# State space mixer: output computed by features, heads in pairs on column halves, decay and skip as loaded tiles

## The chip, the cores and the metric

One core of a Trainium2 chip runs the whole program. The metric is the device time of one execution in microseconds; of several executions the median is taken.

## The reference, cut to what matters

Two transformer-like blocks run one after the other on a sequence of 1024 tokens with 1024 features, all in float32. The second block projects its input to three mixers (attention, a state space mixer, a gated linear recurrence), joins their outputs and projects back. The change is in the state space mixer (SSD): 16 heads of 64 features, in two groups of eight, a state of 128, and the sequence in 8 chunks of 128 tokens.

```
xdt = xh * dt
lmat = exp(where(causal, a_cs[l] - a_cs[s], -inf))        # per head, 128 x 128
cb = einsum('bclgn,bcsgn->bcgls', cc, bc)                 # per group
y_diag = einsum('bcgels,bcsgep->bclgep', cb * lmat, xdt)  # inside the chunk
states = einsum('bclgn,bcgel,bclgep->bcgepn', bc, decay_states, xdt)
y_off = einsum('bclgn,bcgepn,bcgel->bclgep', cc, prev_states, exp(a_cs))  # from earlier chunks
y = y_diag + y_off + xh * d_skip
```

`y` is then gated with silu(z), normalised by groups, and goes with the other mixers' outputs into the last projection.

## The kernel before

**How the work is ordered.** Each stage is a Python generator. Two calls of `weave` (line 146) run the generators against a small planner clock: a generator yields the TensorE time that it has just emitted and a time for which it wants to wait, and the planner takes the first one in its list that is ready. `ssd` stands first in the second list, ahead of `project2`, which emits the remaining big projections (`qkv(1)`, then the gates and the recurrence). So chunks of the mixer are laid between projection matmuls. A tile scheduler may then move an instruction to another place in the order of its engine where its data are ready earlier; each engine and each DMA queue works off its own order.

**Buffers.** Tiles come from pools of fixed slots: 28 `u` (128x1024 float32), 7 `ub` (128x1392), 5 `f` (128x512), 8 PSUM banks, and for weights 3 `raw`, 4 `whi`, 4 `wlo`. `need(...)` lets a generator wait until so many slots are free in the order of emission; a freed slot goes to the end of the list. A weight tile is loaded to `raw` on SP's queue (line 227) and split in a high part (ACT, line 215) and a low part (POOL or DVE, line 212); each wide projection matmul (128x512) is made three times with these parts.

**Before the mixer.** `steps` (1714) computes the step sizes and the running sums `acs` by token, and from them `eacs` (half of exp(acs)), `dtd` and `eend`; it also transposes the sums to `rest` (16 rows per chunk by token) and writes them in parts to DRAM (`seg_l`, `seg_r`). `ssd_tail` (1839) finishes one 128-feature tile of the convolved input at a time: silu, four and four transposes to token order, and for the eight feature tiles of x a write of the token-ordered copy to `xtm_dram` (1859).

**One chunk of `ssd`** (1886 to 1990), token by token order:
- loads: `xt` (128 tokens x 1024 features, 512 KB, line 1896), `rl` and `rr` (1898, 1899); `xdt` = x times the step on POOL (1902), with 32 zeroed columns behind (1901);
- `pcb` (1905) is the product of B and C of each group; `pseg` (1916, 1920) and an exponential on ACT (1921) give the decay matrices `lt`, which DVE multiplies with `pcb` (1924);
- POOL makes `xdec` (1930) and multiplies `xt` by the skip factors in place (1931);
- `pyo` (1939, not in chunk 0): C stationary, the state of eight heads moving, one 128x512 float32 matmul per group; DVE multiplies by `eacs` (1941) and adds the skip part (1943);
- `pyd` (1951): for each head `lt` (128x128) stationary and 96 columns of `xdt` moving, of which 64 are wanted; DVE adds four heads at a time (1953);
- `pst` (1963) updates the state (1966, 1969);
- `pyt2` (1982): eight transposes turn the chunk's 1024 features to feature order, ACT copies them (1983), and ACT's queue writes them to `yraw_dram` (1985).

In the trace a float32 matmul or weight load appears as two records; a transpose as one. Another stage, `sgu_mixer`, already has float32 matmuls with 64 stationary columns and 128 moving ones, whose outputs go by turns to PSUM partitions 0 to 63 and 64 to 127 (line 1084):

```
for j in range(2):
    pe.matmul(p[64 * j:64 * j + 64, n, :], vn[q][:, n, gi * 64:(gi + 1) * 64], swt[:, gi, :],
              start=True, stop=True)
```

Of the kernel before, what the change touches and what calls it, by code (L numbers as in the profile page):

```python
# [75 lines left out]
def tile_block(ctx: ExitStack, tc: tile.TileContext, A, out):  # L76
# [55 lines left out]
    def need(**n):  # L132
        while any(len(C[k].free) < x for k, x in n.items()):
            yield 0.0, 0.7
# [1570 lines left out]


    T_FD, T_XL, T_ZL, T_XBC, T_ZA, T_ZS = 0, 1, 5, 9, 21, 25
    sp = acs = eacs = dtd = eend = None
    negc = const.tile([128, 8, 8], F32, name="negc")
    negc_dram = dr.tile([64, 128], F32, name="negcd")  # L1710
    seg_l = dr.tile([6, 128 * 128], BF16, name="segl")
    seg_r = dr.tile([6, 128 * 128], BF16, name="segr")

    def steps():
        nonlocal sp, acs, eacs, dtd, eend
        sp = small("sp", [128, 8, 24], bufs=2, tag="s5x")
        acs = small("acs", [128, 8, 24], bufs=2, tag="s5x")
        eacs = small("eacs", [128, 8, 16], bufs=2, tag="s5z")
        dtd = small("dtd", [128, 8, 16], bufs=2, tag="s5z")
        eend = small("eend", [128, 8, 16], bufs=1, tag="s5si")  # L1720
        tri = small("tri", [128, 128], tag="s5y")
# [72 lines left out]
        rest = st_[:, 4, 0:128]  # L1794
        v.tensor_copy(rest, pr_[:, 128:256])  # L1795
        free(pr_)
        s.activation(eacs[:], acs[:, :, 8:24], AF.Exp)
        s.activation(eend[:], endb[:, :, 8:24], AF.Exp)
        v.tensor_tensor(dtd[:], endb[:, :, 8:24], acs[:, :, 8:24], op=ALU.subtract)
        s.activation(dtd[:], dtd[:], AF.Exp)  # L1800
        v.tensor_tensor(dtd[:], dtd[:], sp[:, :, 8:24], op=ALU.mult)
        v.tensor_scalar(eacs[:], eacs[:], 0.5, None, op0=ALU.mult)

        sq128 = lambda d, r: d[r].rearrange("(a b) -> a b", a=128)
        for j in range(3):
# [28 lines left out]
        return x  # L1834

    xtm_dram = dr.tile([SEQ, 1024], F32, name="xtm")
    bfm, btm, cfm = {}, {}, {}

    def ssd_tail(i, x):
        yield from need(f=2)  # L1840
        for hf in range(2):
            t = f512("th")
            s.activation(t[:], half(x, hf), AF.Tanh, scale=0.5)
            v.scalar_tensor_tensor(half(x, hf), t[:], 1.0, half(x, hf), op0=ALU.add, op1=ALU.mult)
            free(t)
        yield 0.0, 8.0
        if i < 10:
            yield from need(u=1)
            xs_ = u("xst", (128, 8, 128))
            for q in range(2):  # L1850
                yield from need(ps=1)
                p = bank("ptt", (128, 4, 128))
                for c in range(4):
                    pe.transpose(p[:, c, :], x[:, (4 * q + c) * 128:(4 * q + c + 1) * 128], ident[:])
                s.activation(xs_[:, 4 * q:4 * q + 4, :], p[:], AF.Copy, scale=0.5)
                free(p)
                yield 0.5, 0.0
        if i < 8:
            nc.scalar.dma_start(xtm_dram[:].rearrange("(c p) f -> p c f", p=128)[:, :, i * 128:(i + 1) * 128], xs_[:])
            free(x, xs_)  # L1860
        elif i < 10:
            bfm[i - 8], btm[i - 8] = x, xs_
        else:
            cfm[i - 10] = x
        done.add(f"xbc{i}")
# [20 lines left out]
    def ssd():  # L1886
# [4 lines left out]
        bch = lambda x: x.unsqueeze(2).to_broadcast([128, 16, 64])  # L1891
        for c in range(8):
            tk = slice(c * 128, (c + 1) * 128)
            yield from need(ub=4, u=3, f=1, ps=2)
            xt = ub("xt", (128, 1024))
            nc.sync.dma_start(xt[:], xtm_dram[tk, :])
            rl, rr = ub("rl", (6, 2048), BF16), ub("rr", (6, 2048), BF16)
            nc.sync.dma_start(rl[:], seg_l[:, c * 2048:(c + 1) * 2048])
            nc.sync.dma_start(rr[:], seg_r[:, c * 2048:(c + 1) * 2048])
            xdt = ub("xdt", (128, 1056))  # L1900
            g.memset(xdt[:, 1024:1056], 0.0)
            g.tensor_tensor(h64(xdt[:, 0:1024]), h64(xt[:]), bch(sp[:, c, 8:24]), op=ALU.mult)
            pcb = bank("pcb", (128, 2, 128))
            for gi in range(2):
                pe.matmul(pcb[:, gi, :], bfm[gi][:, tk], cfm[gi][:, tk], start=True, stop=True)
            cb_ = f512("cbs")
            cbs = cb_[:, 0:256].rearrange("p (g l) -> p g l", g=2)
            s.activation(cbs, pcb[:], AF.Copy, scale=0.25)
            free(pcb)
            lt = []  # L1910
            for gi in range(2):
                lt.append(u("lt", (128, 8, 128)))
                for b in range(2):
                    yield from need(ps=1)
# [12 lines left out]
            xdec = None  # L1927
            if c < 7:
                xdec = u("xdec")
                g.tensor_tensor(h64(xdec[:]), h64(xt[:]), bch(dtd[:, c]), op=ALU.mult)  # L1930
            g.tensor_tensor(h64(xt[:]), h64(xt[:]), bch(hrow[:, 2, 8:24]), op=ALU.mult)
            yield 0.5, 6.0
            yield from need(u=1)
            yt = u("yt")
            for gi in range(2):
                if c:
                    yield from need(ps=1)
                    pQ = bank("pyo", (128, 8, 64))
                    pe.matmul(pQ[:].rearrange("p h d -> p (h d)"), cfm[gi][:, tk],
                              state[:, gi].rearrange("p h d -> p (h d)"), start=True, stop=True)  # L1940
                    v.tensor_tensor(h64(half(yt, gi)), pQ[:],
                                    eacs[:, c, 8 * gi:8 * gi + 8].unsqueeze(2).to_broadcast([128, 8, 64]), op=ALU.mult)
                    v.tensor_tensor(half(yt, gi), half(yt, gi), half(xt, gi), op=ALU.add)
                    free(pQ)
                    yield 0.9, 0.0
            for q in range(4):
                yield from need(ps=1)
                pN = bank("pyd", (128, 4, 96))
                for j in range(4):
                    h = 4 * q + j  # L1950
                    pe.matmul(pN[:, j, :], lt[h // 8][:, h % 8, :], xdt[:, h * 64:h * 64 + 96], start=True, stop=True)  # L1951
                yq = h64(yt[:, q * 256:(q + 1) * 256])
                v.tensor_tensor(yq, yq if c else h64(xt[:, q * 256:(q + 1) * 256]), pN[:, :, 0:64], op=ALU.add)
                free(pN)
                if q == 1:
                    yield 1.8, 0.0
            free(xt, xdt, lt)
            yield 1.8, 0.0
            if c < 7:
                for gi in range(2):  # L1960
                    yield from need(ps=1)
                    pS = bank("pst2", (128, 8, 64))
                    pe.matmul(pS[:].rearrange("p h d -> p (h d)"), btm[gi][:, c, :], half(xdec, gi),
                              start=True, stop=True)
                    if c:
                        g.tensor_tensor(state[:, gi], state[:, gi],
                                        eend[:, c, 8 * gi:8 * gi + 8].unsqueeze(2).to_broadcast([128, 8, 64]),
                                        op=ALU.mult)
                        v.tensor_tensor(state[:, gi], state[:, gi], pS[:], op=ALU.add)
                    else:  # L1970
                        v.tensor_copy(state[:, gi], pS[:])
                    free(pS)
                free(xdec)
                yield 1.8, 2.0
            yield from need(u=1)
            ys = u("ys", (128, 8, 128))
            for q in range(2):
                yield from need(ps=1)
                p = bank("pyt2", (128, 4, 128))
                for j in range(4):  # L1980
                    k = 4 * q + j
                    pe.transpose(p[:, j, :], yt[:, k * 128:(k + 1) * 128], ident[:])
                s.activation(ys[:, 4 * q:4 * q + 4, :], p[:], AF.Copy)
                free(p)
            nc.scalar.dma_start(yraw_dram[:].rearrange("(k p) t -> p k t", p=128)[:, :, tk], ys[:])
            free(yt, ys)
            yield 0.9, 0.0
        free(state, *bfm.values(), *btm.values(), *cfm.values())
        done.add("ssd")

# [604 lines left out]
```

## Time and profile before

| | us |
|---|---|
| median of 3 runs | 2401.92 |
| lowest and highest | 2399.53, 2407.82 |
| the profiled execution | 2402.67 |
| its span, first to last instruction | 2400.8 |

The span is what the profile divides into shares. The profiled execution's own time is 1.9 us more than its span and 0.75 us above the median of the runs. `PE` is TensorE's matmuls, `PEld` its weight loads (they lie beside the matmuls), `DVE`, `ACT` and `POOL` the other engines, `SP` a queue that issues DMAs. A matmul record's length includes its way through the array; what matmuls cost one after another is read from the distance of their starts.

### The profile page before, as it was taken

To read this page: it belongs to the slowest core of one execution; us is meant where nothing else is said; L and a number is where in the kernel's file an instruction comes from. 1 tells how busy PE (TensorE), PEld (TensorE's weight loads), DVE (VectorE), ACT (ScalarE), POOL (GpSimd) and SP (SyncE) were. 2 spreads that over 40 slices of the span, in tenths; PEclk is the share of its full clock that TensorE was granted. 3 is DMA by queue.
4 is the path that set the end of the run, shared out by engine and by line. 5 is a ranking of instruction groups with operands and counts; after the bars stand their busy time and mean duration, and the time that the engine had idled before them with its cause. 6 is when DMAs were issued, how large, how long until landed. Compare 5 with 4: busy or idle time off the path is not lost.

```text
span 2400.8 us, 29770 instructions
## 1 busy us (share of the span) xinstructions
PE 2260.8 (94%) x11002; PEld 1795.4 (75%) x11002; DVE 1217.6 (51%) x2148; ACT 795.5 (33%) x1425; POOL 945.5 (39%) x855
## 2 busy tenths in 40 slices
PE   5898789797999999999999998999999999999998
PEld 2787657575678888888888876787777777778877
DVE  8689644886961202021212785766644585662111
ACT  2423222443342121212112354334333354543322
POOL 4465534747553232222324543123652233120543
PEclk7999889799999999999999999999999999999999
DMA  7311444344222111111112334232344433231564
GB/s 270 94 48 58 134 150 158 113 159 140 72 87 66 49 49 46 51 40 53 49 58 83 110 115 145 70 94 88 110 146 144 168 110 136 67 115 63 155 190 141
DMA packets 144194, 251.68 MB, mean 105 GB/s; under 512 B 15720, under 2 KB 51240, under 8 KB 144048
## 3 DMA queue, kind: packets, MB, share of 16 engines
q1 hardware_dynamic: 110960, 209.25, 27.2%
q10 hardware_dynamic: 30816, 32.76, 4.1%
q0 software_dynamic: 2272, 7.77, 1.0%
q8 instruction: 86, 1.41, 0.2%
q14 instruction: 60, 0.49, 0.1%
HBM read 200.20 MB, written 48.48 MB: 104 GB/s over the span
## 4 chain that ended last, share of the span: by engine, by line
PE 69%; DVE 15%; DMA 5%; issue 3%; POOL 3%; ACT 3%; SPq 1%; DVEq 0%; ACTq 0%; POOLq 0%
PE pf L255 6%; PE pf L251 6%; PE pf L253 6%; PE pz L251 6%; PE pz L253 6%; PE pz L255 6%; PE pg L238 3%; PE pg L239 3%; PE pg L240 3%; PE pO L2331 2%; DVE cv L809 2%; PE pfo L238 2%; PE pfo L239 2%; PE pfo L240 2%; PE pyd L1951 1%
## 5 line engine op out<-in xcount | busy, mean ns | idle before, releaser
L212 POOL TENSOR_TENSOR wlo<-raw,whi 128x512 fp32r<-128x512 f32 (+1 forms) x285 | 397.3, 1396 | 868.0 <-ACT whi L215 839.2
L215 ACT ACTIVATE whi<-raw 128x512 fp32r<-128x512 f32 (+1 forms) x432 | 267.0, 622 | 1019.0 <-PE pf L253 295.1
L212 DVE TENSOR_TENSOR wlo<-raw,whi 128x512 fp32r<-128x512 f32 (+1 forms) x147 | 115.9, 789 | 364.8 <-ACT whi L215 364.4
L255 PE MATMUL pf<-h,wlo 128*128 128x512 f32 x704 | 231.8, 392 | 5.2 <-DVE wlo L212 2.9
L251 PE MATMUL pf<-h,whi 128*128 128x512 f32 x704 | 231.9, 392 | 0.1
L253 PE MATMUL pf<-h,whi 128*128 128x512 f32 x704 | 231.9, 392 | 0.0
L251 PE MATMUL pz<-u,whi 128*128 128x512 f32 x512 | 170.1, 399 | 0.9 <-DVE sptmp L1795 0.6
L253 PE MATMUL pz<-u,whi 128*128 128x512 f32 x512 | 168.2, 394 | 0.0
L255 PE MATMUL pz<-u,wlo 128*128 128x512 f32 x512 | 166.8, 394 | 0.0
L255 PEld LDWEIGHTS pf<-h,wlo 128*128 128x128 f32 x704 | 132.5, 188 | 36.0 <-DVE wlo L212 3.7
L251 PEld LDWEIGHTS pf<-h,whi 128*128 128x128 f32 x704 | 132.4, 188 | 29.6 <-ACT whi L215 0.5
L253 PEld LDWEIGHTS pf<-h,whi 128*128 128x128 f32 x704 | 132.5, 188 | 29.3
L239 PE MATMUL pg<-wlo,act 128*128 128x512 f32 x352 | 138.3, 393 | 0.9 <-DVE wlo L212 0.5
L238 PE MATMUL pg<-whi,act 128*128 128x512 f32 x352 | 137.1, 393 | 0.4 <-ACT whi L215 0.4
L240 PE MATMUL pg<-whi,act 128*128 128x512 f32 x352 | 137.0, 392 | 0.0
L251 PEld LDWEIGHTS pz<-u,whi 128*128 128x128 f32 x512 | 95.8, 188 | 24.5 <-issue 1.9
L253 PEld LDWEIGHTS pz<-u,whi 128*128 128x128 f32 x512 | 96.0, 188 | 22.3 <-issue 1.2
L255 PEld LDWEIGHTS pz<-u,wlo 128*128 128x128 f32 x512 | 96.0, 188 | 21.9 <-issue 0.7
L1579 DVE TENSOR_TENSOR x<-x,pg 128x512 f32<-128x512 f32 x80 | 53.7, 685 | 109.3 <-PE pg L240 109.2
L239 PE MATMUL pfo<-wlo,mix 128*128 128x512 f32 x256 | 101.1, 396 | 0.5 <-POOL wlo L212 0.5
L1552 DVE TENSOR_TENSOR a<-a,pf 128x512 f32<-128x512 f32 x44 | 28.7, 683 | 143.0 <-PE pf L255 143.0
L240 PE MATMUL pfo<-whi,mix 128*128 128x512 f32 x256 | 100.5, 394 | 0.0
(641 smaller groups left out, 4968.9 us busy)
## 6 DMA issues: line engine op xcount, KB each, us to landing
raw<-in_w_ffn_in_dram SPq DMA_DIRECT2D x108, 256.0 KB
wm<-in_w_mod_dram SPq DMA_DIRECT2D x48, 512.0 KB
raw<-in_w_out_dram SPq DMA_DIRECT2D x96, 256.0 KB
raw<-in_w2f_dram SPq DMA_DIRECT2D x66, 256.0 KB
raw<-in_w_ffn_out_dram SPq DMA_DIRECT2D x56, 256.0 KB
raw<-in_w2q_dram SPq DMA_DIRECT2D x48, 256.0 KB
raw<-in_w_in_dram SPq DMA_DIRECT2D x36, 256.0 KB
mraw<-y2d SPq DMA_DIRECT2D x32, 256.0 KB
```

The lines of the kernel that those rows point to most:

```text
L212: (v if dve else g).tensor_tensor(lo, full, hi, op=ALU.subtract)
L215: s.activation(hi, full, AF.Copy)
L238: pe.matmul(p, lh, rh, start=start, stop=False)
L239: pe.matmul(p, lh, rl, start=False, stop=False)
L240: pe.matmul(p, ll, rh, start=False, stop=stop)
L251: pe.matmul(p, wh, xh[k], start=k == 0, stop=False)
L253: pe.matmul(p, wh, xl[k], start=False, stop=False)
L255: pe.matmul(p, wl, xh[k], start=False, stop=k == kt - 1)
L809: v.scalar_tensor_tensor(a3, *tap(k), a3, op0=ALU.mult, op1=ALU.add)
L1552: v.tensor_tensor(a_[:], a_[:], pair[1][hf][:], op=ALU.mult)
L1579: v.tensor_tensor(x, x, p[t][:], op=ALU.add)
L2331: pe.matmul(pO[:, b, :], x[:, jb % 2, b * 128:(b + 1) * 128], H["va"][:, o:o + 96], start=False, stop=jb == nj - 1 and b == 3)
```

## The change

The stationary and the moving operand change places, so that a chunk's result comes out with features on partitions and tokens along the row. `pyd` has 64 columns of `xdt` stationary and `lt` (128 tokens) moving; the two heads of a 128-feature tile write PSUM partitions 0 to 63 and 64 to 127. `pyo` becomes four matmuls of 128 state columns against C. The transposes and their copies go. The decay factor and the skip part are now needed with features on partitions: `steps` writes half of exp of the transposed sums to `ea_dram`, and each chunk loads `eb` from it (two DMAs that repeat 16 rows over 64 partitions each); `ssd_tail` scales the feature-ordered x by half the skip factor on ACT and writes it to `xd_dram`, and each chunk loads `xd`. A chunk asks for 6 `ub` slots, before 4.

```diff
@@ steps
-        s.activation(eacs[:], acs[:, :, 8:24], AF.Exp)
+        er = small("ear", [128, 128], tag="s5y")
+        s.activation(er[:], rest, AF.Exp)
+        v.tensor_scalar(er[:], er[:], 0.5, None, op0=ALU.mult)
+        nc.scalar.dma_start(ea_dram[:], er[:])
...
-        v.tensor_scalar(eacs[:], eacs[:], 0.5, None, op0=ALU.mult)
@@ before ssd_tail
+    dcol = const.tile([128, 8], F32, name="dcol")
+    for r in range(2):
+        v.tensor_scalar(dcol[64 * r:64 * r + 64, :], hrow[64 * r:64 * r + 64, 2, 8 + r:24:2], 0.5, None, op0=ALU.mult)
@@ ssd_tail
+            s.activation(x[:], x[:], AF.Copy, scale=dcol[:, i:i + 1])
+            nc.scalar.dma_start(xd_dram[i * 128:(i + 1) * 128, :], x[:])
@@ ssd
-            yield from need(ub=4, u=3, f=1, ps=2)
+            yield from need(ub=6, u=3, f=1, ps=2)
...
-            xdt = ub("xdt", (128, 1056))
-            g.memset(xdt[:, 1024:1056], 0.0)
-            g.tensor_tensor(h64(xdt[:, 0:1024]), h64(xt[:]), bch(sp[:, c, 8:24]), op=ALU.mult)
+            xdt = ub("xdt", (128, 1024))
+            xd, eb = ub("xd", (128, 8, 128)), ub("eb", (128, 8, 128))
+            nc.sync.dma_start(xd[:], xd_dram[:].rearrange("(k p) t -> p k t", p=128)[:, :, tk])
+            if c:
+                for r in range(2):
+                    nc.sync.dma_start(eb[64 * r:64 * r + 64], ea_dram[c * 16 + r:c * 16 + 16:2, :].unsqueeze(0)
+                                      .to_broadcast([64, 8, 128]))
+            g.tensor_tensor(h64(xdt[:]), h64(xt[:]), bch(sp[:, c, 8:24]), op=ALU.mult)
...
-            g.tensor_tensor(h64(xt[:]), h64(xt[:]), bch(hrow[:, 2, 8:24]), op=ALU.mult)
...
-                    pQ = bank("pyo", (128, 8, 64))
-                    pe.matmul(pQ[:].rearrange("p h d -> p (h d)"), cfm[gi][:, tk],
-                              state[:, gi].rearrange("p h d -> p (h d)"), start=True, stop=True)
-                    v.tensor_tensor(h64(half(yt, gi)), pQ[:],
-                                    eacs[:, c, 8 * gi:8 * gi + 8].unsqueeze(2).to_broadcast([128, 8, 64]), op=ALU.mult)
-                    v.tensor_tensor(half(yt, gi), half(yt, gi), half(xt, gi), op=ALU.add)
+                    pQ = bank("pyo", (128, 4, 128))
+                    for j in range(4):
+                        pe.matmul(pQ[:, j, :], state[:, gi, 2 * j:2 * j + 2].rearrange("p h d -> p (h d)"),
+                                  cfm[gi][:, tk], start=True, stop=True)
+                    v.tensor_tensor(yt[:, 4 * gi:4 * gi + 4], pQ[:], eb[:, 4 * gi:4 * gi + 4], op=ALU.mult)
                     free(pQ)
                     yield 0.9, 0.0
+                g.tensor_tensor(yt[:], yt[:], xd[:], op=ALU.add)
-            for q in range(4):
+            for gi in range(2):
                 yield from need(ps=1)
-                pN = bank("pyd", (128, 4, 96))
+                pN = bank("pyd", (128, 4, 128))
                 for j in range(4):
-                    h = 4 * q + j
-                    pe.matmul(pN[:, j, :], lt[h // 8][:, h % 8, :], xdt[:, h * 64:h * 64 + 96], start=True, stop=True)
-                yq = h64(yt[:, q * 256:(q + 1) * 256])
-                v.tensor_tensor(yq, yq if c else h64(xt[:, q * 256:(q + 1) * 256]), pN[:, :, 0:64], op=ALU.add)
+                    for r in range(2):
+                        h = 8 * gi + 2 * j + r
+                        pe.matmul(pN[64 * r:64 * r + 64, j, :], xdt[:, h * 64:h * 64 + 64], lt[gi][:, 2 * j + r, :],
+                                  start=True, stop=True)
+                y_ = slice(4 * gi, 4 * gi + 4)
+                v.tensor_tensor(yt[:, y_], yt[:, y_] if c else xd[:, y_], pN[:], op=ALU.add)
                 free(pN)
-                if q == 1:
-                    yield 1.8, 0.0
-            free(xt, xdt, lt)
-            yield 1.8, 0.0
+                yield 0.9, 0.0
+            free(xt, xdt, lt, xd, eb)
+            nc.scalar.dma_start(yraw_dram[:].rearrange("(k p) t -> p k t", p=128)[:, :, tk], yt[:])
...
-            ys = u("ys", (128, 8, 128))
-            for q in range(2):
-                p = bank("pyt2", (128, 4, 128))
-                for j in range(4):
-                    k = 4 * q + j
-                    pe.transpose(p[:, j, :], yt[:, k * 128:(k + 1) * 128], ident[:])
-                s.activation(ys[:, 4 * q:4 * q + 4, :], p[:], AF.Copy)
-            nc.scalar.dma_start(yraw_dram[:].rearrange("(k p) t -> p k t", p=128)[:, :, tk], ys[:])
-            free(yt, ys)
-            yield 0.9, 0.0
+            free(yt)
+            yield 0.1, 0.0
```

## Rows read from the trace of the kernel before

**Rows 1.** The page: busy time by engine, and the granted clock in 40 slices.

```profile
PE 2260.8 (94%) x11002; PEld 1795.4 (75%) x11002; DVE 1217.6 (51%) x2148; ACT 795.5 (33%) x1425; POOL 945.5 (39%) x855
...
PEclk7999889799999999999999999999999999999999
```

**Rows 2.** Busy time by stretch; after POOL come granted clock, DMA share, GB/s.

```profile
core 0: us, PE busy (x) PEld busy (x) DVE busy (x) ACT busy (x) POOL busy (x), PEclk, DMA share, GB/s
1637.00:1820.00 183.00, 182.47 (x986) 137.38 (x986) 98.62 (x142) 62.56 (x114) 94.25 (x80) 1.00 0.37 117
1820.00:2000.00 180.00, 177.72 (x737) 137.87 (x736) 120.50 (x123) 84.64 (x123) 53.15 (x40) 1.00 0.42 146
```

**Rows 3.** TensorE's waits in 1637 to 1820 us: us, times, longest.

```profile
PE pq L238 <- ACT cbs L1908: 0.5, 1, 0.5
```

**Rows 4.** The chain of waits, 1560 us to the end: start, us, what.

```profile
1674.25 3.54 PE pyd L1951 x32
...
1737.29 1.72 PE pyo L1939 x4
```

**Rows 5.** TensorE's timeline in chunk 1: start, us, line, operation, tiles.

```profile
1674.09 3.71 PE L1951 MATMUL pyd<-xdt,lt 128*128 128x96 f32 x32
1677.63 0.38 PE L1916 MATMUL pseg<-mask,identb 128*128 128x512 bf16 x1
...
1682.85 1.03 PE L1982 MATMUL pyt<-ident,yt 128*128 128x128 f32 x8
1683.64 0.47 PE L240 MATMUL pq<-whi,u 128*128 128x512 f32 x1
1683.96 0.39 PE L238 MATMUL pq<-whi,u 128*128 128x512 f32 x1
1684.18 0.60 PE L1905 MATMUL pcb<-xc 128*128 128x128 f32 x4
1684.55 0.48 PE L239 MATMUL pq<-wlo,u 128*128 128x512 f32 x1
1684.87 0.39 PE L240 MATMUL pq<-whi,u 128*128 128x512 f32 x1
```

**Rows 6.** Lines 1951 and 1982: count, duration ns min/median/max, first and last start.

```profile
L1951 PE MATMUL pyd<-xdt,lt x256: 243/275/275, 1651.9 to 1808.5; 128*128 128x96 f32 x128
...
L1982 PE MATMUL pyt<-ident,yt x64: 270/272/327, 1660.9 to 1812.8; 128*128 128x128 f32 x64
```

**Rows 7.** TensorE's timeline around line 1084, and that line's weight loads.

```profile
400.60 0.61 PE L255 MATMUL pz<-hh,wlo 128*128 128x512 f32 x2
401.15 1.09 PE L1084 MATMUL psg<-sw,vn 128*64 128x128 f32 x16
...
403.15 1.09 PE L1084 MATMUL psg<-sw,vn 128*64 128x128 f32 x16
404.18 0.73 PE L251 MATMUL pz<-hh,whi 128*128 128x512 f32 x2
404.75 0.62 PE L253 MATMUL pz<-hl,whi 128*128 128x512 f32 x2
...
L1084 PEld LDWEIGHTS psg<-sw,vn x64: 132/137/137, 401.1 to 410.1; 128*64 128x64 f32 x64
```

**Rows 8.** Groups of ACT, DVE, POOL in 1637 to 1820 us: busy, mean ns, idle.

```profile
L1983 ACT ACTIVATE ys<-pyt 128x512 f32<-128x512 f32 x16 | 8.8, 596 | 6.4 <-PE pyt L1982 6.4
...
L1943 DVE TENSOR_TENSOR yt<-yt,xt 128x512 f32<-128x512 f32 x14 | 15.0, 1080 | 2.7 <-POOL xt L1931 2.2
...
L1931 POOL TENSOR_TENSOR xt<-xt,hrow 128x1024 f32<-128x1024 f32 x7 | 14.2, 2028 | 0.2
...
L212 POOL TENSOR_TENSOR wlo<-raw,whi 128x512 fp32r<-128x512 f32 x20 | 25.8, 1295 | 54.7 <-ACT whi L215 54.7
```

**Rows 9.** SP's queue in 1637 to 1820 us, what it waited for: us, times, longest.

```profile
SPq L227 <- POOL wlo L212: 60.7, 16, 12.3
...
SPq L1896 <- PE pyd L1951: 6.2, 1, 6.2
```

**Rows 10.** DMA queue that ACT issues to, 1637 to 1820 us: packets, MB, share of 16 engines.

```profile
q10 hardware_dynamic: 9472, 6.31, 11.2%
```

More of the change, by code (lines that the diff above doesn't have):

```diff
@@ L1707, in tile_block @@
     T_FD, T_XL, T_ZL, T_XBC, T_ZA, T_ZS = 0, 1, 5, 9, 21, 25
-    sp = acs = eacs = dtd = eend = None
+    sp = acs = dtd = eend = None
     negc = const.tile([128, 8, 8], F32, name="negc")
@@ L1714, in steps @@
     def steps():
-        nonlocal sp, acs, eacs, dtd, eend
+        nonlocal sp, acs, dtd, eend
         sp = small("sp", [128, 8, 24], bufs=2, tag="s5x")
         acs = small("acs", [128, 8, 24], bufs=2, tag="s5x")
-        eacs = small("eacs", [128, 8, 16], bufs=2, tag="s5z")
         dtd = small("dtd", [128, 8, 16], bufs=2, tag="s5z")
@@ L1836, in tile_block @@
     xtm_dram = dr.tile([SEQ, 1024], F32, name="xtm")
+    xd_dram = dr.tile([1024, SEQ], F32, name="xd")
+    ea_dram = dr.tile([128, 128], F32, name="ea")
+    dcol = const.tile([128, 8], F32, name="dcol")
+    for r in range(2):
+        v.tensor_scalar(dcol[64 * r:64 * r + 64, :], hrow[64 * r:64 * r + 64, 2, 8 + r:24:2], 0.5, None, op0=ALU.mult)
     bfm, btm, cfm = {}, {}, {}
@@ L1930, in ssd @@
                 g.tensor_tensor(h64(xdec[:]), h64(xt[:]), bch(dtd[:, c]), op=ALU.mult)
-            g.tensor_tensor(h64(xt[:]), h64(xt[:]), bch(hrow[:, 2, 8:24]), op=ALU.mult)
             yield 0.5, 6.0
             yield from need(u=1)
-            yt = u("yt")
-            for gi in range(2):
-                if c:
+            yt = u("yt", (128, 8, 128))
+            if c:
+                for gi in range(2):
                     yield from need(ps=1)
-                    pQ = bank("pyo", (128, 8, 64))
-                    pe.matmul(pQ[:].rearrange("p h d -> p (h d)"), cfm[gi][:, tk],
-                              state[:, gi].rearrange("p h d -> p (h d)"), start=True, stop=True)
-                    v.tensor_tensor(h64(half(yt, gi)), pQ[:],
-                                    eacs[:, c, 8 * gi:8 * gi + 8].unsqueeze(2).to_broadcast([128, 8, 64]), op=ALU.mult)
-                    v.tensor_tensor(half(yt, gi), half(yt, gi), half(xt, gi), op=ALU.add)
+                    pQ = bank("pyo", (128, 4, 128))
[3 more added lines that the diff above has]
+                    v.tensor_tensor(yt[:, 4 * gi:4 * gi + 4], pQ[:], eb[:, 4 * gi:4 * gi + 4], op=ALU.mult)
@@ L1944, in ssd @@
                     free(pQ)
                     yield 0.9, 0.0
-            for q in range(4):
+                g.tensor_tensor(yt[:], yt[:], xd[:], op=ALU.add)
+            for gi in range(2):
                 yield from need(ps=1)
-                pN = bank("pyd", (128, 4, 96))
+                pN = bank("pyd", (128, 4, 128))
                 for j in range(4):
-                    h = 4 * q + j
-                    pe.matmul(pN[:, j, :], lt[h // 8][:, h % 8, :], xdt[:, h * 64:h * 64 + 96], start=True, stop=True)
-                yq = h64(yt[:, q * 256:(q + 1) * 256])
-                v.tensor_tensor(yq, yq if c else h64(xt[:, q * 256:(q + 1) * 256]), pN[:, :, 0:64], op=ALU.add)
+                    for r in range(2):
[4 more added lines that the diff above has]
+                v.tensor_tensor(yt[:, y_], yt[:, y_] if c else xd[:, y_], pN[:], op=ALU.add)
@@ L1974, in ssd @@
                 yield 1.8, 2.0
-            yield from need(u=1)
-            ys = u("ys", (128, 8, 128))
-            for q in range(2):
-                yield from need(ps=1)
-                p = bank("pyt2", (128, 4, 128))
-                for j in range(4):
-                    k = 4 * q + j
-                    pe.transpose(p[:, j, :], yt[:, k * 128:(k + 1) * 128], ident[:])
-                s.activation(ys[:, 4 * q:4 * q + 4, :], p[:], AF.Copy)
-                free(p)
-            nc.scalar.dma_start(yraw_dram[:].rearrange("(k p) t -> p k t", p=128)[:, :, tk], ys[:])
-            free(yt, ys)
-            yield 0.9, 0.0
+            free(yt)
+            yield 0.1, 0.0
         free(state, *bfm.values(), *btm.values(), *cfm.values())
```

## The prediction

> **What bounds the kernel now.** I read the page first: TensorE is busy for 94% of the span, no other engine for more than 51%, and its granted clock is at nine tenths or more in all of the last 32 slices [rows 1]. An average over stages proves little, so the stretch of the chunks comes next: in 1637 to 1820 us TensorE is busy for 182.47 of 183 us at a granted clock of 1.00, the 2.4 GHz level, and in the 180 us behind it for 177.72 [rows 2]. The view of waits agrees: in the stretch TensorE waits once, for 0.5 us [rows 3]. And the chain of waits runs through the mixer's own matmuls at their full length [rows 4]. So the reader is to see a stage that is simply full of matmuls: the mixer's chunks are laid between the projections, and every microsecond of matmul taken out moves all that follows forward, as long as nothing new makes TensorE wait.
>
> **The change part by part.** First TensorE, since its time is the path.
>
> *Transposes, removed.* A chunk's eight start at 1682.85, the next matmul at 1683.64, and that one then takes 0.32 us to the start of its successor where a wide one takes 0.22 (1683.96 to 1684.18) [rows 5]: 0.79 + 0.10 = 0.89 us. There are 64, eight per chunk [rows 6]: 8 x 0.89 = 7.1 us gone.
>
> *The heads' products.* Today the 32 records of a chunk (16 heads, two each [rows 6]) run from 1674.09 to 1677.63, 3.54 us [rows 5], and all of it lies on the chain [rows 4]: 0.11 us a record. The new form is in the trace already, in another stage: 64 stationary columns, 128 moving, float32, outputs by turns on either half of the partitions. Sixteen such records start at 403.15 and the next matmul at 404.18, 1.03 us [rows 7]; at 0.11 a record, one after the other, they would take 1.76. So the two halves do run side by side. The change of form costs something: two wide matmuls before such a run take 0.55 us (400.60 to 401.15), two behind it 0.57 (404.18 to 404.75), where two cost 0.44 [rows 5]; about 0.1 going in and 0.1 coming out. A chunk has two runs of 16. Emitted back to back they cost 2 x 1.03 + 0.2 = 2.3, of which the seam, counted in both, gives back about 0.1: 2.2 us. The generator keeps its turn between them (its wait is 0.0), so I take this. Saved: 3.54 - 2.2 = 1.34 a chunk, 10.7 us over eight. Bounds: with projections always between the runs 2 x 1.25 = 2.5, so 8.3 us; with no cost of the change of form 2.06, so 11.8 us.
>
> *The state's part.* Today 1.72 us a chunk [rows 4]. Then eight 128x128 float32 matmuls, 16 records. The nearest row: four records of that shape start at 1684.18, the next matmul at 1684.55, which then takes 0.32 instead of 0.22 [rows 5], 0.45 us for four with what they leave behind. Sixteen: 1.8 us, plus one such exit for each group of eight: about 1.87. Added: 0.15 x 7 chunks = 1.0 us (bounds 0 and 1.5).
>
> Sum on TensorE: 7.1 + 10.7 - 1.0 = 16.8 us.
>
> *The other engines*, which cost nothing while TensorE is the bound. ACT loses 16 copies of 0.6 us and gains eight of twice the width, estimated at 1.2 us each from that row [rows 8], in the stage before: even. DVE loses 14 additions [rows 8]; its four quarter additions become two of half width; the multiplication by the decay stays. POOL loses 1.9 to 2.0 us a chunk for the skip product [rows 8] and gains an addition of the same size, 128x1024. Two small operations on the skip factors at the start and one in `steps` are under 0.3 us together beside other work. The cover for all this is that TensorE is full and these engines are not: DVE is busy for 98.62 and POOL for 94.25 of the 183 us [rows 2]. Without the cover POOL's addition would cost up to 2 us a chunk; that is a rival below.
>
> *Transfers.* Each chunk also loads `xd` (512 KB) and, from the second, `eb` (2 x 256 KB); before it there are eight writes of 512 KB. The loads go in pieces of 512 bytes: 8 x 1024 + 14 x 512 = 15,360 pieces. ACT's queue, which moves mostly pieces of about that size, took 11.2% of the 16 engines over 183 us for 9,472 packets [rows 10], so the new ones take about 18% beside a share of 37% [rows 2]: there is room. On SP's queue it is 22 more issues; behind them wait the weight loads. SP mostly waits for a free `raw` buffer, that is, it is ahead of need: 60.7 us in 16 waits for POOL's low parts alone [rows 9].
>
> *Slots.* A chunk wants 6 of 7 `ub` slots. The two staging tiles of `qkv(1)` take such slots when they are free, and then the next chunk is emitted later, after other work: projections move ahead of the chunk, and TensorE has them to do. I cost this at nothing; if it made the mixer end behind the projections that cover it, each of its waits would show.
>
> What comes next once 17 us are gone: the stage stays full of matmuls, and what follows starts as much earlier. The profiled execution took 2402.67 us; 2402.67 - 16.8 = 2385.9. It stands 0.75 above the median of 2401.92, so by the median 2385.1. I forecast 2386, with one microsecond for small waits.
>
> **The rivals.**
>
> *Slower: SP held up by the new loads.* With 6 of 7 slots per chunk the slots rotate onto what the previous chunk still reads: `xd` lands where `xdt` was, free only after the last `pyd`; `eb` lands where `xd` was, free only after DVE's last addition. SP works in order, so weight loads issued behind wait too. For it: already today SP waits for `pyd` once, 6.2 us [rows 9]. Against it: that wait cost TensorE nothing [rows 3]. The point from which it decides: three `raw` and four split tiles lie ahead, and a tile of the token projections is 12 matmuls of 0.22 [rows 5], 2.6 us; four of them are 10.6 us. A block of 15 us per chunk would leave TensorE idle for 4 us, seven times: 28 us, and 2385 + 28 = 2413.
>
> *POOL's addition on the path.* It waits for DVE's second product, which waits for `pyo`; DVE's next addition waits for POOL, and behind it stand low parts of weights. If all of its 1.9 us reached TensorE in seven chunks, 13.3 us go back: 2385 + 13 = 2398. For it: POOL's rows show low parts as its largest group [rows 8]. Against it: in those 1.9 us TensorE has the heads' products, 2.2 us, to do.
>
> *The halves run one after the other*, so the change doesn't do what it says: 32 records at 0.11 are 3.54 again, only the transposes pay, 7.1 - 1.0 = 6.1, and the time is 2396. Rows 7 speak against it.
>
> *Weight loads of the halves are not hidden.* Half a load's columns take 137 ns [rows 7]. If they stood between the products, a pair of records would take 0.11 + 0.137 = 0.25 us, 16 pairs 4.0 a chunk, 0.4 more than now: 7.1 - 1.0 - 3.5 = 2.6 us gained, 2399. The rows speak against it: eight pairs in 1.03 us are 0.13 each [rows 7]. The Trainium skill, page "TensorE: Matmul & The Clock Gate", section "The mechanism" (under packing small matmuls), says that a weight load runs beside matmuls under way only where their row groups differ; two column halves share all rows, so by it the loads would be exposed. The trace disagrees in this shape, 0.13 us a pair, so the measurement decides.
>
> **How the numbers follow.** Forecast 0.75; slower by SP 0.09; POOL's addition 0.09; halves in turn 0.04; loads exposed 0.03. The forecast's own range is the sum's bounds, 8.3 + 7.1 - 1.5 = 13.9 and 11.8 + 7.1 = 18.9 us, that is 2383 to 2388, widened by the order: a planner with other yields lays the stages behind in another way, and TensorE has 2.3 us of gaps in the 180 us behind the mixer [rows 2], so a few microseconds to either side: 2377 to 2392. The range reaches on to the two cases with small gains: 2377 to 2399. Left out: the slower case and the far ends, under 2 in 10. A measurement of this kernel can tell about 0.3% from no change, 7 us, so faster means under 2394.7. Faster: the forecast and a share of the POOL case that costs only half, 0.75 + 0.03 = 0.78. Within 0.3%: what is left of POOL's case, the halves in turn and exposed loads, 0.13. Slower 0.09.
>
> **What would show it.** Right: `pyd` has 256 records of 64 stationary columns whose starts come in pairs a few ns apart, a chunk's 32 in about 2.2 us; the transposes' line is gone; TensorE is still busy for over 98% of the mixer's stretch; the mixer's last chunk ends some 15 us earlier or with more projection work done. Wrong: records of `pyd` 0.11 us apart one by one; TensorE waiting for low parts of weights or for weight loads in the stretch; SP waiting for `pyd` or DVE for over 10 us per chunk; the stretch full, but the time lost again in the stages behind.

## The result and the profile after

| | us |
|---|---|
| changed kernel, median of 6 runs (lowest, highest) | 2377.55 (2372.7, 2379.33) |
| kernel before, 6 runs beside them | 2402.03 (2396.09, 2407.82) |
| ratio, with its 95% interval | 0.9894 [0.9876, 0.9912] |
| profiled execution after, its span | 2377.7, 2376.0 |

The change gains 24.5 us by the medians, where 16 had been forecast. 2377.55 lies at the lower edge of the range, and 0.9894 of the 2401.92 it started from, 2376.5, just below it. The interval of the ratio is a gain of 21 to 30 us. The sign and the place were right; the size was not. Of one_half's six runs, below, one took 2505.63 us at a granted clock of 0.855 where the others had 0.97 and is left out of its median.

The page of the changed kernel, busy time by engine and the granted clock, answers to [rows 1]:

```profile
PE 2240.9 (94%) x11022; PEld 1782.9 (75%) x11022; DVE 1196.1 (50%) x2120; ACT 794.1 (33%) x1417; POOL 941.3 (40%) x846
...
PEclk7999989799999999999999999999999999999999
```

Its busy time by stretch answers to [rows 2]:

```profile
1634.40:1820.00 185.60, 184.92 (x1103) 141.96 (x1103) 86.71 (x119) 58.44 (x106) 96.99 (x76) 1.00 0.60 175
1823.00:2000.00 177.00, 172.22 (x717) 132.91 (x716) 128.04 (x141) 92.54 (x135) 57.11 (x47) 0.99 0.42 146
```

The stretch of the chunks is as full as before, 184.92 of 185.60 us at a granted clock of 1.00. So the gain is fewer microseconds of matmul, and the stretch must have become shorter. To measure it, I take two marks that both kernels share: the last transpose `ptt` ahead of the chunks and the first matmul `plg` of the recurrence behind them. The lines of these two tiles, before the change (count, duration ns min/median/max, first and last start):

```profile
L1854 PE MATMUL ptt<-ident,xc x80: 270/272/273, 1514.7 to 1626.2; 128*128 128x128 f32 x80
...
L2101 PE MATMUL plg<-xc,lgw x32: 591/592/697, 1848.0 to 1989.5; 128*128 128x512 f32 x32
```

and after it:

```profile
L1861 PE MATMUL ptt<-ident,xc x80: 270/272/273, 1512.4 to 1624.0; 128*128 128x128 f32 x80
...
L2105 PE MATMUL plg<-xc,lgw x32: 590/592/697, 1823.2 to 1967.3; 128*128 128x512 f32 x32
```

From 1626.2 to 1848.0 is 221.8 us, from 1624.0 to 1823.2 is 199.2: 22.6 us less. From the first `plg` to the end of the span it is 552.8 us in both (2400.8 - 1848.0 and 2376.0 - 1823.2). So nothing is gained behind the second mark: 22.6 us lie between the marks, and 2.2 ahead of the first, which before_again takes up below.

Where it comes from inside, by adding the distances from each matmul's start to the next one's:

| us in the stretch | before | after | difference | forecast |
|---|---|---|---|---|
| heads' products `pyd`, with the wide matmul's delay behind them | 28.4 | 15.5 | -12.9 | -10.7 |
| transposes, with the same | 7.2 | 0 | -7.2 | -7.1 |
| state's part `pyo`, with the same | 12.1 | 13.2 | +1.1 | +1.0 |
| wait of the first `plg` | 2.0 | 0 | about -2.2 | none |
| all else | | | about -1.4 | none |

The wait's 2.2 is read from starts too, in TensorE's timeline before:

```profile
1844.91 0.61 PE L255 MATMUL pz<-u,wlo 128*128 128x512 f32 x2
1845.37 0.62 PE L251 MATMUL pz<-u,whi 128*128 128x512 f32 x2
1848.00 1.55 PE L2101 MATMUL plg<-xc,lgw 128*128 128x512 f32 x3 [2.01 <-DVE xc L1832]
```

`plg` follows two matmuls from 1845.37 after 2.63 us, where two take 0.46. The last row of the table is what is left of 22.6.

**The heads' products.** TensorE's timeline in chunk 1 after the change answers to [rows 5]:

```profile
1651.78 0.39 PE L240 MATMUL pq<-whi,u 128*128 128x512 f32 x1
1652.01 1.05 PE L1953 MATMUL pyo<-xc,state 128*128 128x128 f32 x8
1652.99 1.97 PE L1966 MATMUL pyd<-lt,xdt 128*64 128x128 f32 x32
1654.89 0.50 PE L238 MATMUL pq<-whi,u 128*128 128x512 f32 x1
1655.23 0.39 PE L239 MATMUL pq<-wlo,u 128*128 128x512 f32 x1
```

The 32 records take 1654.89 - 1652.99 = 1.90 us, where they took 3.54 [rows 5]. The line's weight loads and matmuls, as in [rows 6, 7]:

```profile
L1966 PEld LDWEIGHTS pyd<-lt,xdt x256: 132/137/137, 1653.0 to 1811.8; 128*64 128x64 f32 x128
L1966 PE MATMUL pyd<-lt,xdt x256: 272/273/323, 1653.0 to 1811.9; 128*64 128x128 f32 x128
```

32 loads of 137 ns would be 4.4 us one after the other; they fit into 1.90, beside the products and beside each other. In the chain of waits, as in [rows 4], a later chunk reads:

```profile
1730.04 1.78 PE pyo L1953 x16
1731.82 1.90 PE pyd L1966 x32
1733.72 1.91 PE pst L1978 x4
```

**The recurrence's wait.** TensorE's waits between the marks, before (beside the one of [rows 3]):

```profile
PE plg L2101 <- DVE xc L1832: 2.0, 1, 2.0
```

after:

```profile
PE pseg L1930 <- ACT cbs L1922: 0.7, 1, 0.7
```

`plg` needs DVE's convolution `xc`. Before, DVE began its last tile ahead of `plg` at 1840.87, 7.1 us ahead; the DVE timeline of before:

```profile
1840.87 1.28 DVE L1830 TENSOR_SCALAR xc<-xp,cols 128x1024 f32<-128x1024 f32 x1 [1.67 <-ACT xp L1827]
1842.19 5.75 DVE L1832 SCALAR_TENSOR_TENSOR xc<-xp,cols,xc 128x1024 f32<-128x1024 f32 x3
```

After, the same steps lie between 1810.0 and 1818.3, five microseconds ahead of `plg` at 1823.2. Projections have moved ahead of the chunks: the last matmul of `qkv` starts at 1729.6 where it started at 1768.2, and the gates and the recurrence's preparation follow earlier. Behind the second mark a later `plg` waits for DVE 0.9 us where it waited 0.3; the way from the mark to the end is 552.8 us in both all the same.

**SP.** Some of its waits in 1634 to 1823 us, as in [rows 9]:

```profile
SPq L227 <- POOL wlo L212: 53.1, 17, 5.7
...
SPq L1914 <- POOL yt L1958: 3.9, 3, 1.7
...
SPq L1911 <- DVE yt L1955: 2.6, 1, 2.6
```

Lines 1911 and 1914 are the new loads of `xd` and `eb`. They do wait for slots that the chunk before still uses, though mostly for other readers than the prediction named: `pyd` holds `xd` up for 0.5 us in all and DVE's last addition `eb` for 0.2. No such wait is longer than 2.6 us, and TensorE waits once in the whole stretch, 0.7 us, for ACT.

### The profile page after: what moved, and what is told of

The parts are those of the page before. It is cut to its first block, busy times and chain, and to the rows that moved or that the text cites. A ratio compares the mean times of both kernels' runs of the same rounds, so it can differ in the third digit from the quotient of the medians.

```text
span 2376.0 us, 29812 instructions
## 1 busy us (share of the span) xinstructions
PE 2240.9 (94%) x11022; PEld 1782.9 (75%) x11022; DVE 1196.1 (50%) x2120; ACT 794.1 (33%) x1417; POOL 941.3 (40%) x846
## 4 chain that ended last, share of the span: by engine, by line
PE 64%; DVE 16%; DMA 7%; issue 4%; POOL 4%; ACT 3%; SPq 1%; ACTq 0%; POOLq 0%; DVEq 0%
PE pf L253 6%; PE pf L255 6%; PE pf L251 6%; PE pz L251 5%; PE pz L253 5%; PE pz L255 5%; PE pg L238 3%; PE pg L239 3%; PE pg L240 3%; PE pO L2335 2%; DVE cv L809 2%; PE pfo L238 2%; PE pfo L239 2%; PE pfo L240 2%; POOL wlo L212 1%
## 5 line engine op out<-in xcount | busy, mean ns | idle before, releaser
L255 PEld LDWEIGHTS pz<-u,wlo 128*128 128x128 f32 x512 | 95.9, 188 | 22.4 <-issue 1.2
```

The lines of the kernel that those rows point to most:

```text
L255: pe.matmul(p, wl, xh[k], start=False, stop=k == kt - 1)
```

## The experiments

The stretch is the distance between the same two marks throughout. Each ratio is against runs of the kernel before beside it, whose medians were 2400.73 to 2402.19 us.

| | median us | ratio [95%] | stretch |
|---|---|---|---|
| before | 2402.03 | 1 | 221.8 |
| before_again | 2397.59 (one run) | | 221.9 |
| changed kernel | 2377.55 | 0.9894 [0.9876, 0.9912] | 199.2 |
| after_again | 2376.82 | 0.9896 [0.9877, 0.9916] | 198.8 |
| halves_in_blocks | 2381.35 | 0.9915 [0.9895, 0.9935] | 203.6 |
| transposes_back | 2388.89 | 0.9947 [0.9928, 0.9966] | 208.7 |
| halves_alone | 2391.78 | 0.9957 [0.9941, 0.9973] | 209.1 |
| one_half | 2390.00 | 0.9957 [0.9943, 0.9971] | 212.9 |
| loads_once | 2375.35 | 0.9894 [0.9879, 0.9908] | 198.6 |
| state_halves | 2377.69 | 0.9916 [0.9896, 0.9936] | 201.0 |

**after_again**: the changed kernel as it is, for a second trace.

> The changed kernel once more, as the measure for the runs beside it. My theory: its gain is TensorE time in the mixer's stretch, 12.9 us from the heads' products, 7.2 from the transposes, minus 1.1 for the state's part, 19.0 in all; the other 5 us or so of the 24.5 are waits and the course of the run, so they vary: 19 to 25 us below the kernel before. Rival (the whole gain is fixed by the new order of the work): 24 to 25 us again, with the first matmul of the attention stage 22 us earlier again and the first block's end 2 us earlier again.

2376.82 us, and a stretch of 198.8 us: the two traces of the changed kernel agree to 0.4 us there. It is 24.9 us below the kernel before, which lies in both expected ranges, so the time does not tell the theory from the rival. The first mark does in part: it stands at 1625.4 here, 1.4 us later than in the first trace, so the lead with which the mixer began does not repeat. Differences of the stretch are taken against 199.0, the mean of the two.

**halves_in_blocks**: in the changed kernel, all of one half's products of a bank ahead of the other half's.

```diff
-                for j in range(4):
-                    for r in range(2):
+                for r in range(2):
+                    for j in range(4):
```

> The changed kernel with the loops over tile and half exchanged: four heads on the lower half of the columns, then four on the upper. Same products, loads, buffers and transfers. Theory (the two halves running side by side are the source): records of the heads' products no longer start in pairs but 0.109 us apart, a chunk's 32 cost about 3.5 to 3.6 us instead of 1.9, 13 us over eight chunks are given back: 2389 to 2391 against 2377.5. Rival (half as many stationary columns to load, or features in place of tokens, is what pays): at most 3 us slower than the changed kernel.

2381.35 us: a loss of 4.5 against after_again, and 4.6 in the stretch. This expectation was missed: the order costs a third of what it should if the halves ran in the order of the program. The chain of waits, a later chunk:

```profile
1733.03 1.78 PE pyo L1953 x16
1734.82 2.50 PE pyd L1966 x32
1737.31 1.91 PE pst L1978 x4
```

A chunk's products take 2.50 us, between 1.90 by turns and the 3.5 of one after the other. How that comes about, by line 1966 alone in stretches of half a microsecond of that chunk (stretch, its length, PE busy with the number of records in brackets, PEld the same, clock, DMA; a record counts in each stretch that it touches):

```profile
1734.70:1735.20 0.50, 0.45 (x4) 0.46 (x5) 1.00 1.02 393
1735.20:1735.70 0.50, 0.50 (x10) 0.50 (x9) 1.00 1.03 399
1735.70:1736.20 0.50, 0.50 (x12) 0.50 (x9) 1.00 1.04 404
```

and the same view of the changed kernel in chunk 1:

```profile
1652.95:1653.45 0.50, 0.46 (x8) 0.46 (x10) 1.00 0.81 254
1653.45:1653.95 0.50, 0.50 (x14) 0.50 (x12) 1.00 0.31 111
```

and of one_half (next experiment), where all products lie on one half:

```profile
1735.25:1735.75 0.50, 0.50 (x7) 0.50 (x5) 1.00 1.00 341
```

By turns, products run two at a time from the first. In blocks, the first 0.45 us hold four records where they held eight, and then the rate climbs to 12. Within a half, records follow at 0.11 us (one_half), so the climb means that products of the other half started ahead of products that stand before them in the program. In order, four blocks of eight records 0.109 us apart need at least 4 x 7 x 0.109 = 3.05 us from the first start to the last, more than the whole 2.50. By single starts the second block begins 0.49 us behind the first (1735.24 and 1734.75), when five of the first block's eight records have started. A record does not name its half, but the scheduler has not reordered them: in this run's program the four lower products of every bank stand ahead of its four upper ones, as the loops have them, in all eight chunks.

**one_half**: in the changed kernel, every head's product goes to partitions 0 to 63. The upper half of the features gets no product inside the chunk: that part of the computation is left out.

```diff
-                        pe.matmul(pN[64 * r:64 * r + 64, j, :], xdt[:, h * 64:h * 64 + 64], lt[gi][:, 2 * j + r, :],
+                        pe.matmul(pN[0:64, j, :], xdt[:, h * 64:h * 64 + 64], lt[gi][:, 2 * j + r, :],
                                   start=True, stop=True)
...
-                v.tensor_tensor(yt[:, y_], yt[:, y_] if c else xd[:, y_], pN[:], op=ALU.add)
+                v.tensor_tensor(yt[0:64, y_], yt[0:64, y_] if c else xd[0:64, y_], pN[0:64], op=ALU.add)
+                if not c:
+                    g.tensor_copy(yt[64:128, y_], xd[64:128, y_])
```

> The changed kernel with the heads' products of both halves written to the lower 64 PSUM partitions, so that all 16 heads of a chunk use the same half of the columns; the sum for the upper 64 features of each tile is left out (DVE adds on 64 partitions, and POOL copies the skip part there in the first chunk). Same count, shapes and loads. The run with the halves in blocks cost 4.5 us only, with its records partly overlapped (20.5 us in all against 15.3). Theory (side by side is the whole source of the heads' gain): no two records overlap, starts 0.109 us apart, 256 records in 28 us, 12.6 us more than in the changed kernel, 2388 to 2391. Rival (the form with 64 stationary columns is cheaper by itself): records closer than 0.109, total below 24 us, under 2386.

2390.00 us, as expected, and 13.9 us in the stretch. The chain:

```profile
1733.01 1.78 PE pyo L1953 x16
1734.79 3.64 PE pyd L1966 x32
1738.43 1.91 PE pst L1980 x4
```

The products took 29.25 us in all, where 28 were expected and 15.3 were taken by turns: 13.9 more, all of the loss. 64 stationary columns alone are no cheaper than 128 were, 3.64 us against 3.54 [rows 4]. The gain of the heads' products is two halves at once and nothing else.

**transposes_back**: the changed kernel, and behind each chunk eight transposes of `yt` and two copies on ACT, as they stood before, into a tile that nothing reads.

```diff
-            free(yt)
-            yield 0.1, 0.0
+            yield from need(u=1)
+            ys = u("ys", (128, 8, 128))
+            for q in range(2):
+                yield from need(ps=1)
+                p = bank("pyt2", (128, 4, 128))
+                for j in range(4):
+                    pe.transpose(p[:, j, :], yt[:, 4 * q + j, :], ident[:])
+                s.activation(ys[:, 4 * q:4 * q + 4, :], p[:], AF.Copy)
+                free(p)
+            free(yt, ys)
+            yield 0.9, 0.0
```

> The changed kernel with eight transposes of the chunk's result and two copies on ACT put back at the end of each chunk; nothing reads the copies. Theory: TensorE is full in this stretch, so 64 transposes of 0.109 us and their exits cost what they cost before, 7 us: 2384 to 2385. Rival (the stretch has slack, the transposes were hidden): 2376 to 2379.

2388.89 us, 12.1 more than after_again, against some 7 to 8 expected. The stretch grew by 9.7: the transposes 7.5, the delay of the matmuls behind them 0.5, and 1.8 of waits, which TensorE's waits show:

```profile
PE pyt L1996 <- DVE yt L1969: 1.8, 2, 1.6
```

DVE's last addition is shortly ahead of the transposes in this kernel. So where nothing waits the transposes cost 8.0 us here, with the delay behind them, and 7.2 in the kernel before, near the forecast's 7.1; the 2.4 us that lie outside the stretch are within what the stages ahead of it vary from run to run (before_again, below).

**halves_alone**: the kernel before, with the heads' products alone on halves; `pyo` and the transposes stay, and DVE adds the products' feature-ordered copy behind the transposes. Since `yt` and `xt` change roles in chunk 0, `tm` is the token-ordered one of them and `fm` the other; `ys` lies in `fm`.

```diff
-                pN = bank("pyd", (128, 4, 96))
+                pN = bank("pyd", (128, 4, 128))
                 for j in range(4):
-                    pe.matmul(pN[:, j, :], lt[h // 8][:, h % 8, :], xdt[:, h * 64:h * 64 + 96], start=True, stop=True)
+                    for r in range(2):
+                        h = 8 * gi + 2 * j + r
+                        pe.matmul(pN[64 * r:64 * r + 64, j, :], xdt[:, h * 64:h * 64 + 64], lt[gi][:, 2 * j + r, :],
+                                  start=True, stop=True)
+                v.tensor_copy(ys[:, 4 * gi:4 * gi + 4], pN[:])
...
-                    pe.transpose(p[:, j, :], yt[:, k * 128:(k + 1) * 128], ident[:])
-                s.activation(ys[:, 4 * q:4 * q + 4, :], p[:], AF.Copy)
+                    pe.transpose(p[:, j, :], tm[:, k * 128:(k + 1) * 128], ident[:])
+                v.tensor_tensor(ys[:, 4 * q:4 * q + 4, :], ys[:, 4 * q:4 * q + 4, :], p[:], op=ALU.add)
```

> The kernel before with the heads' products alone on column halves: the state's part and the skip stay by tokens, the transposes stay and turn them, DVE adds the two (it gains 1.1 us of work a chunk, ACT loses its copies); no new loads, no new slots. Theory: 12.9 us below the kernel before, 2388 to 2391. Rival (the gain needs the whole change, since the new adds by DVE and the late transposes hold TensorE up): less than 6 us below the kernel before.

2391.78 us, 0.8 above what was expected and 10 less than before, and 12.7 less in the stretch. The heads' products take 1.90 us here too; the chain and, behind it, TensorE's waits:

```profile
1731.82 1.72 PE pyo L1939 x4
1733.54 1.90 PE pyd L1954 x32
...
1741.03 0.87 PE pyt L1981 x8
```

```profile
PE plg L2100 <- DVE xc L1832: 2.5, 1, 2.5
```

The recurrence's wait is still there. So the heads' products give 12.7 without help from the other parts. With 9.7 for the transposes that is 22.4, near the whole of 22.6, but the agreement is partly chance: 1.8 of the 9.7 is a wait that transposes_back alone has, and neither number holds the state's part (+1.1) or the recurrence's wait (-2.2).

**loads_once**: in the changed kernel, `xd` and `eb` are loaded once, for chunk 1, and every chunk uses these. The other chunks' own skip part and decay are left out; of 15,360 pieces of load 2,048 remain.

```diff
+        yield from need(ub=2)
+        xd, eb = ub("xd", (128, 8, 128)), ub("eb", (128, 8, 128))
+        nc.sync.dma_start(xd[:], xd_dram[:].rearrange("(k p) t -> p k t", p=128)[:, :, 128:256])
+        for r in range(2):
+            nc.sync.dma_start(eb[64 * r:64 * r + 64], ea_dram[16 + r:32:2, :].unsqueeze(0)
+                              .to_broadcast([64, 8, 128]))
         for c in range(8):
...
-            yield from need(ub=6, u=3, f=1, ps=2)
+            yield from need(ub=4, u=3, f=1, ps=2)
...
-            xd, eb = ub("xd", (128, 8, 128)), ub("eb", (128, 8, 128))
-            nc.sync.dma_start(xd[:], xd_dram[:].rearrange("(k p) t -> p k t", p=128)[:, :, tk])
...
```

> The changed kernel with the decay and skip tiles loaded once before the first chunk and held; every chunk then uses those of chunk 1, so the others' decay and skip are left out. Seven loads of 512 KB and twelve of 256 KB go, with their places on SP's queue and the slots' rotation. Theory (transfers are covered while TensorE is full): DMA share of the stretch falls from 0.60 to about 0.45, TensorE's stretch and the time stay, 2373 to 2380. Rival (the new loads take part of the gain back by holding up SP and the weights): 5 us or more faster, 2372 or less.

2375.35 us and a stretch of 198.6: the loads cost nothing that can be told from none. The stretch by busy time:

```profile
1634.00:1820.00 186.00, 186.00 (x1109) 143.09 (x1109) 89.28 (x119) 58.53 (x106) 97.53 (x76) 1.00 0.42 136
```

The DMA engines' share falls from 0.60 to 0.42, so the loads are 0.18 of it, and TensorE, full in both, does not notice.

**before_again**: the kernel before, for a second trace.

> The kernel before, unchanged, for a second trace. Theory: the stretch from the last transpose of the convolved input to the recurrence's first matmul takes 221 us again, with a wait of some 2 us for DVE at its end, while the stage ahead of it begins and ends up to 3 us earlier or later than in the first trace. Rival (the 2 us that the changed kernel is ahead when its mixer begins belong to the change): the last transpose starts at 1626 us again, not below 1625.

The same two marks, in this trace:

```profile
L1854 PE MATMUL ptt<-ident,xc x80: 270/272/273, 1512.0 to 1623.5; 128*128 128x128 f32 x80
...
L2101 PE MATMUL plg<-xc,lgw x32: 591/592/697, 1845.4 to 1986.6; 128*128 128x512 f32 x32
```

The stretch is 221.9, as in the first trace, but it begins at 1623.5 and not at 1626.2. The stages ahead of it vary by 2.7 us from run to run, so the two microseconds by which the changed kernel's stretch began earlier in its first trace lie within what the kernel before does by itself. They are there already at the first `ptt` (1514.7 in the first trace of before, 1512.0 here, 1512.4 in the changed kernel), ahead of the edited parts of `steps` and `ssd_tail`.

**state_halves**: in the changed kernel, the state's part on halves too, for a kernel that might beat both.

```diff
                     for j in range(4):
-                        pe.matmul(pQ[:, j, :], state[:, gi, 2 * j:2 * j + 2].rearrange("p h d -> p (h d)"),
-                                  cfm[gi][:, tk], start=True, stop=True)
+                        for r in range(2):
+                            pe.matmul(pQ[64 * r:64 * r + 64, j, :], state[:, gi, 2 * j + r, :], cfm[gi][:, tk],
+                                      start=True, stop=True)
```

> The changed kernel with the state's part on column halves too: for each head 64 state columns stationary, outputs by turns on either half, so a chunk's 16 head products and 16 state products have one form and TensorE doesn't change it between them. Theory (a pair of halves steps 0.109 us, a full-width record 0.112, and a change of form costs about 0.1): the state's part falls from 13.2 us to about 12.3 in the stretch, about 1 us in all, too little for the times to show: 2374 to 2379. Rival (twice as many products cost twice as much issue): the state's part rises above 14 us and the time by 2 us or more.

2377.69 us, 0.9916 [0.9896, 0.9936]: no better than the changed kernel. The state's part falls from 13.2 us to 12.7 and not to 12.3. The chain:

```profile
1728.92 1.90 PE pyo L1954 x32
1730.82 1.75 PE pyd L1967 x32
```

The change of form moves from `pyd` to `pyo`: 1.90 + 1.75 = 3.65 us against 1.78 + 1.90 = 3.68. Where the stationary operand fills all 128 columns, halves have nothing to share. The stretch is 201.0, and TensorE waits once there, 2.9 us for ACT, where the changed kernel waited 0.7. No version that computes everything beat the changed kernel.

## Why the prediction was right in kind and wrong in size

**The heads' term was the step that failed.** It read "Emitted back to back they cost 2 x 1.03 + 0.2 = 2.3 ... 2.2 us". A run's 1.03 us of [rows 7] is 8 pairs at 0.109, 0.87, and a fixed part of 0.16 for the first pair and for the way from the last pair to the next matmul. Two runs emitted back to back are one run, 16 x 0.109 + 0.16 = 1.90, which is what the timeline measures; doubling took the 0.16 twice and gave back 0.1. The 0.2 on top is the delay of the neighbours. It lies outside the 1.03, but most of it was no addition. The way in, 0.09 us (0.20 from the last `pyo` to the first `pyd`, where two `pyo` lie 0.11 apart), is held by the row of `pyo`, whose forecast had an exit of its own. The wide matmul behind takes 0.34 us (1654.89 to 1655.23), but behind the old products it took 0.32 already, as the timeline of before shows:

```profile
1697.81 1.03 PE L1951 MATMUL pyd<-xdt,lt 128*128 128x96 f32 x8
1698.62 0.48 PE L238 MATMUL pq<-whi,u 128*128 128x512 f32 x1
1698.94 0.40 PE L239 MATMUL pq<-wlo,u 128*128 128x512 f32 x1
1699.17 0.40 PE L240 MATMUL pq<-whi,u 128*128 128x512 f32 x1
```

So the saving was 1.64 us in a chunk as in [rows 5] and not 1.34; over all eight, with the delay of the matmuls behind, 12.9 and not 10.7, outside even the bound of 11.8, which had doubled the 1.03 too.

**The recurrence's wait was in the rows and not in the sum.** The "2.3 us of gaps" behind the mixer [rows 2] were allowed to widen the range by the order, but not to be gained. 2.0 of them were one wait, of `plg` for DVE, and it went. That it went because projections moved ahead is argued from the order in the two traces; which part of the change makes the planner do so was not tried alone. It is 2.5 us in halves_alone, which asks for the same slots as before, and nought in every kernel built on the changed one, transposes_back included, so it is not the missing transposes.

**The rest.** 16 us were forecast. 2.2 more came from the heads, 2.2 from the wait, 1.4 from small differences that were not followed up, and 0.9 had been held back "for small waits" and the like: 22.7, the stretch. The medians' 24.5 holds some 2 us more, as much as the stages ahead vary by, and the interval of 21 to 30 us holds both.

**What was right.** TensorE was the bound and stayed it: 184.92 of 185.60 us. The transposes gave 7.2 for 7.1. The state's part took 1.1 for 1.0, but by luck in part, since its working does not come out: four records and their exit are 0.37 + 0.10 = 0.47 us in [rows 5] and not 0.45, and 1.8 with two exits of 0.1 is 2.0 and not 1.87. Measured were 1.89 a chunk. The move of projections ahead of chunks, costed at nothing, came, and cost nothing. Transfers reached a share of 0.60 where 0.55 had been added up. The small DVE operations took 0.55 us, not under 0.3, beside other work.

**The rivals.** SP held up by the new loads: its waits for them were 2.6 us at the longest, and loads_once gained nothing. POOL's addition: DVE waited for it once, 1.9 us, and TensorE never. The halves one after the other: 1.90 us a chunk, and one_half shows what the other case costs, 13.9 us. Weight loads not hidden: a pair would have taken 0.25 us and a chunk 4.0; it took 1.90. In one_half, where all products share their columns too, loads of 137 ns were hidden as well, at 0.11 us a record. The Trainium skill, page "TensorE: Matmul & The Clock Gate", section "The mechanism", says that a load runs beside matmuls under way only where row groups differ; two column halves share their rows, and the trace disagrees. The same section also lets a load for a background weight buffer go ahead, which the prediction left out; that would fit these rows, but no run here tests it.

## What to carry to other kernels

A matmul that fills only half the array's columns can be made in pairs, on either half by turns: here that took 46% off its time (3.54 to 1.90 us), while the same 64 columns on one half alone gained nothing. When a cost is read from a run of another stage, split it into a rate and a fixed part before multiplying, since a run's length holds its entry and exit already. A gap behind the changed stage belongs into the sum's bounds as a possible gain, with the name of what it waits for.

## What the runs showed of the hardware

- **The order of the halves matters less than expected.** In blocks, a chunk's products took 2.50 us and not 3.64: TensorE starts products of the free half ahead of products that stand before them in the program. The Trainium skill, page "TensorE: Matmul & The Clock Gate", section "The mechanism", says that matmuls start and end strictly in program order; the rate of 12 records in half a microsecond, against 7 in one_half, and 2.50 us where order needs 3.05 at least, speak against it for starts on different column halves.
- **The change of form is small.** In chunk 1 the last `pyo` starts 0.20 us ahead of the first `pyd`, where two of them lie 0.11 apart: 0.09 going in. The run itself holds 0.16 more than its 16 pairs at 0.109. The delay of the wide matmul behind, 0.34 us where the next takes 0.22, is hardly the form's: it was 0.32 behind the old products, which filled all 128 columns.
- **The stretch repeats, the stages ahead of it do not.** Two traces of one kernel agreed in the stretch to 0.1 us (before) and 0.4 us (changed), while its start moved by 2.7 and 1.4 us. Marks around the edited stage told differences of a microsecond that the medians, with runs some 6 to 14 us apart, could not.
